# Twelve tiles of a feed-forward product in two blocks of seven products, added into DRAM by the output pairs

## The chip, the cores and the metric

The kernel runs on one core of one Trainium2 chip. The metric is the device time of one execution in microseconds (us); the median of three runs is compared. Engines are named as in the profile: PE is TensorE, PEld its weight loads, DVE is VectorE, ACT is ScalarE, POOL is GpSimd, SP is SyncE. SP and POOL both issue DMAs, each on a queue of its own (q1 for SP, q0 for POOL).

## The reference, cut to what matters

One layer of a diffusion backbone over 512 latent tokens of width 1024: a token mixer, a gated residual, then a SwiGLU feed-forward block (FFN) with a gated residual, and a last RMS norm. The change lies in the FFN alone:

```python
D_FF = -(-8 * D_MODEL // (3 * 256)) * 256        # 2816 = 22 tiles of 128

def _swiglu(h, w_in, w_out):
    g, u = jnp.split(h @ w_in, 2, axis=-1)
    return (jax.nn.silu(g) * u) @ w_out

x = x + g2 * _swiglu(_modulate(x, norm_ffn[l], sh2, sc2), w_ffn_in[l], w_ffn_out[l])
return _rmsnorm(x, norm_final)
```

The first product makes 22 tiles of g and 22 of u, the second sums the 22 tiles of silu(g) * u into 8 output tiles of 128 rows and 512 tokens.

## The kernel before, in words

Activations lie with channels on the 128 partitions and the 512 tokens along the free axis. To keep fp32 accuracy each operand is split into a high and a low fp32r half, and a product of two tiles is three matmuls: high by high, high by low, low by high (`mm3`, lines 191 to 193). `mm3_low_last` (L198 to L201) does the same sums with the low weights at the end.

**Block products.** A tile pair, g_j above u_j, by the 512 tokens in two halves of 256 is a 2 x 2 block product. It is done with seven block products instead of eight, in the manner of Strassen and Winograd, from sums of weight blocks (A11, S1, S2, A12, S3, S4, A22) and sums of the token halves (11, N1, N2, 21, T3, 22, T4). Class `Pair` issues them: `front` does A11, S1, S2, A12, and `back` does S3, S4, A22. With 8 tiles of input width each block product is 4 x 3 matmuls of 256 columns, 84 for a pair. Between A11 and S2 ScalarE copies one PSUM bank to another (L1091).

`prepare` makes a pair's weights ready: two loads by SP, into `ur` (two buffers, L1021) and `wr` (three buffers, L1022), then sums on DVE (L1054 to L1062), casts and splits on ACT and DVE (L1034, L1036, L1044, L1045). Blocks named in `sent` get their low half another way: ACT writes the negated high half (L1038) and an accumulating DMA on POOL's queue adds the weight from DRAM (`ol<-in_wffi`, L1039). `Even` and `Odd` are pairs whose results are not only split but also summed and split again, so that two tiles of silu(g) * u serve as the block operand of the second product; there are three buffers (`bo`) for three such double tiles. `Out` is a pair of output tiles: the seven block products of two of the eight output rows by six tiles, 7 x 3 x 3 = 63 matmuls of 256 columns. Its results are scaled by the gate and written to DRAM by POOL's queue (L1247, L1251).

`run` interleaves the items: while one item's front runs, the back of the item before is woven in, and the next item's weights are prepared. Where an Out follows an Odd (`joint`), the order is different, since the Out's operands are only just being made. Outside the parts with an order written by hand (`manual_schedule`), a planner orders each engine's instructions; `issue_after` holds one back until another has been issued.

**Stages of the FFN before.**

1. Tiles 0 to 2 as plain products, then pairs 3 to 7.
2. First part of the second product: each of 8 output tiles sums tiles 0 to 7, 24 matmuls of 512 columns, with weights of 1024 columns loaded, cast and split (`wchunk`, L161, L162). The result is added to the residual `x1` (L1432), and x1 goes to the DRAM tile `x1d` (L1455, L1470).
3. Even and Odd pairs for tiles 8 to 13, then four Outs. An Out writes into the DRAM tile `od`.
4. Plain pairs 14 to 21. Meanwhile `also` adds od to x1d, row by row, by accumulating DMAs from DRAM to DRAM on POOL's queue (L1487).
5. The tail: x1 is read back from x1d (L1524), each output tile sums tiles 14 to 21 in two token halves, 24 matmuls of 256 columns each, and squares are summed (L224 to L231) for the last norm, which multiplies (L1514) and stores.

The last pair's tile is put off in stage 2 and in the tail: output 0 (in the tail the first two) begins with the other tiles.

Of the kernel before, what the change touches and what calls it, by code (L numbers as in the profile page):

```python
# [10 lines left out]
F32 = mybir.dt.float32  # L11
F32R = mybir.dt.float32r
AF = mybir.ActivationFunctionType
ALU = mybir.AluOpType
# [3 lines left out]
P = 128  # L18
D = 1024
KT = D // P  # L20
T = 512
# [29 lines left out]
def layer_kernel(ctx: ExitStack, tc, xT, cT, w0, w1, wv0, wv, wada_a, wada_b, par, crow, bg, wpool,  # L51
                 wout, wffi, wffo, icnt, consts, out):
    nc = tc.nc
# [7 lines left out]
    def open_pool(name, tags, side="left"):  # L61
        st = ExitStack()
        p = st.enter_context(tc.tile_pool(name=name, bufs=1, side=side, reuse_waits="tile"))
        pools[name] = p
        for t in tags:
            homes[t] = p
        stacks[name] = st

    def close_pool(name):
        stacks.pop(name).close()  # L70

    def tl(tag, shape, dtype=F32, bufs=1, align=None):
        cnt[0] += 1
        return homes[tag].tile(shape, dtype, name=f"{tag}_{cnt[0]}", tag=tag, bufs=bufs, align_bytes=align)

    def S(tag, dtype=F32):
        return tl(tag, [P, T], dtype, bufs[tag], HALFLINE if tag in shifted else LINE)

    ps = ctx.enter_context(tc.tile_pool(name="ps", bufs=4, space=PSUM))
    dram = ctx.enter_context(tc.tile_pool(name="dram", bufs=1, space=DRAM))  # L80
# [127 lines left out]
    class SumSq:  # L208
# [4 lines left out]
        def __init__(self, urgent=()):  # L213

            self.urgent = urgent
            self.n = {}
            self.last = {}
# [58 lines left out]
    def mod_rows(k):  # L276

        raw = tl("ada", [P, KT, 256], F32, 3)
        nc.sync.dma_start(raw.rearrange("p k c -> p (k c)"), wada_a[k])
        acc = PS()  # L280
        for r in range(2):
            for g in range(4):
                nc.tensor.matmul(acc[32 * g:32 * g + 32, :256], sil[:, 4 * r + g, :], raw[:, 4 * r + g, :],
                                 start=r == 0, stop=r == 1, tile_position=(0, 32 * g))
        rows = S("tmp")
        nc.scalar.copy(rows[:, :256], acc[:, :256])
        return rows
# [83 lines left out]
    rows = mod_rows(0)  # L371
# [5 lines left out]
    rows = mod_rows(1)  # L377
# [5 lines left out]
    for k in range(KT):  # L383
        parts = ((0, 0), (0, 1), (1, 0))[0 if k else 1:]
        products(k, 0, nf // 2, parts)
        if k + 2 < KT:
            rows = mod_rows(k + 2)
# [598 lines left out]
    def norm_tiles(c, r, at, also=lambda k: None):  # L986
        t = norm_first(0, c, r)
        for k in range(KT):
            t = norm_rest(k, c, t, at(k), lambda: norm_first(k + 1, c, r) if k < KT - 1 else None)
            also(k)  # L990
# [80 lines left out]
    class Pair:  # L1071
# [5 lines left out]
        begun, f, behind = False, None, None  # L1077
# [53 lines left out]
        def second(self, y):  # L1131
            s = self.s[:, TC:]
            nc.scalar.activation(s, y, AF.Silu)
            V.scalar_tensor_tensor(s, self.q[:, TC:], -1.0, s, ALU.mult, ALU.mult)

        def fourth(self, x):
            s = self.s[:, :TC]
            V.scalar_tensor_tensor(s, x, -1.0, s, ALU.mult, ALU.mult)
            self.done()
# [73 lines left out]
    class Out(Pair):  # L1213
# [3 lines left out]

        def __init__(self, j, turn, evens, c0, c1):
            super().__init__(j, turn)
            self.evens, self.c, self.into = evens, slice(c0 * P, c1 * P), od[c0]  # L1220

        def prepare(self):
            w = [wffo[2 * self.j + e][:, self.c] for e in range(2)]
# [20 lines left out]

        def second(self, y):
            self.scaled(self.o[:, TC:], y, g2)
            nc.gpsimd.dma_start(self.into[2 * self.j], self.o)  # L1247

        def fourth(self, x):
            self.scaled(self.o1[:, :TC], x, ng2)  # L1250
            nc.gpsimd.dma_start(self.into[2 * self.j + 1], self.o1)  # L1251

    def made(it):
        for _ in it.prepare():
# [2 lines left out]
    def run(items, also=lambda it: None):  # L1257

        prev, casts[:] = None, []
        for it, after in zip(items, items[1:] + [None]):  # L1260
            f = it.f = it.f or it.front()
            if after:
                made(after)
            b = prev.back() if prev else iter(())
            joint = isinstance(it, Out) and not isinstance(prev, Out)
            if joint:
                next(b)
            if not it.begun:
                next(f)
                if joint:  # L1270
                    next(b)
                next(f)
            if casts:
                with tc.issue_after(it.copied.ins):
                    casts.pop().cast(0, 4)
            if joint:
                next(b)
                after.f = after.front()
                next(after.f)
                next(after.f)  # L1280
                after.begun = True
            next(b, None)
            next(f)
            next(b, None)
            next(f)
            next(b, None)
            also(it)
            prev = it
# [2 lines left out]
    ng2 = small([P, KT], "ng2")  # L1291
    V.tensor_scalar(ng2, g2, -1.0, None, ALU.mult)
    x1d = dram.tile([KT, P, T], F32, name="x1d")
    od = {c0: dram.tile([KT, P, T], F32, name=f"od{c0}") for c0 in (8,)}

    for j in range(NW, KT):
        proj_out(j, wo[j], HALF[0])
# [51 lines left out]
    with tc.manual_schedule(engines={mybir.EngineType.PE, mybir.EngineType.Activation, mybir.EngineType.DVE}):  # L1349
# [7 lines left out]
        f = Half(1, HALF[0])  # L1357
# [19 lines left out]
        f = Half(1, HALF[1])  # L1377
# [20 lines left out]
        f = Half(2, HALF[1])  # L1398
# [42 lines left out]

    starts = (8,)
    turn = itertools.count(NP + 1)
    plain = [third] + [Pair(j, next(turn)) for j in range(NP + 1, starts[0])]
    plain[1].behind = third.p["low"]
# [3 lines left out]
    c1 = starts[0]  # L1451
# [4 lines left out]
    items, ins = [], []  # L1456
    for c0 in starts:
        evens = []
# [6 lines left out]
    c0, c1 = starts[-1] + 6, FT  # L1465
    plain = [Pair(j, next(turn)) for j in range(c0, c1)]
# [4 lines left out]
    close_pool("late4")  # L1471
    close_pool("late0")
    open_pool("late0", ("bo", "nf", "ev"))
    rows = iter([(c, j) for c in starts for j in range(KT)])

    def also(it):
        if it is plain[0]:
            close_pool("late0")
            open_pool("late0", ("act", "before_act", "x1"))
            tl("before_act", [P, NEXT], F32, 1, LINE)  # L1480
            shifted.add("act")
            bufs["act"] = 2 * (c1 - c0)
            x1[:] = [S("x1") for _ in range(KT)]
        if it in plain[:-2]:
            with tc.issue_after(items[items.index(it) + 1].p["added"].ins):
                for c, j in itertools.islice(rows, 1 + (it in plain[1:3])):
                    nc.gpsimd.dma_start(x1d[j], od[c][j], accum_op=ALU.add, max_dma_last_dim=2048)  # L1487

    for _ in run(items, also=also).back():
        pass  # L1490
# [145 lines left out]
```

## Time and profile before

| what | value |
|---|---|
| median of 3 runs | 884.06 us (883.71 to 884.94) |
| the profiled execution's own time | 883.43 us |
| its span, first to last instruction | 881.6 us |
| PE busy | 870.8 us (99%) |
| DVE, ACT, POOL busy | 631.2, 454.2, 82.6 us |
| first part of the second product (tiles 0 to 7) | 616.9 to 660.4 us |
| Even and Odd pairs and Outs (tiles 8 to 13) | 660.4 to about 754 us |
| plain pairs 14 to 21, up to the tail | up to 826.5 us |
| tail, up to the last residual's product | 826.5 to 871.1 us |
| DMA: mean rate, and POOL's queue q0 | 147 GB/s; 8032 packets, 16.26 MB |

Times in the profile count from the first instruction. "L1091" is line 1091 of the kernel. In the view of windows a row gives a stretch, its length, the busy time and count of each engine in it, the granted clock, the mean busy share of the 16 DMA engines and the rate. In a timeline a row is start, duration, engine, line, operation, out<-in, and in brackets the idle time before and what ended it. The starts of two matmuls in a row tell their pace, as they overlap.

### The profile page before, as it was taken

The page shows a single profiled execution, that of the slowest core. Times are in us where ns is not written, and L with a number is a line of the kernel's source. Part 1 is how long each engine was busy: PE and PEld are TensorE (multiplying, and loading weights), DVE is VectorE, ACT ScalarE, POOL GpSimd, SP SyncE. Part 2 cuts the span into 40 slices and gives each one's busy share as a digit, 9 for nine tenths or more (in the row PEclk, how much of TensorE's full clock was granted, in tenths as well). Part 3 has the DMA queues.
Part 4 walks back from the last instruction along what each step waited for, and adds up shares of the span by engine and source line. Part 5 has one row for each costly group of instructions (what it writes and reads, how often), then busy time and mean ns, then how long its engine had stood idle before and what let it go on. Part 6 is the DMA issues. An engine that isn't in the chain of part 4 may idle for free.

```text
span 881.6 us, 15517 instructions
## 1 busy us (share of the span) xinstructions
PE 870.8 (99%) x6052; PEld 800.4 (91%) x6052; DVE 631.2 (72%) x1232; ACT 454.2 (52%) x867; POOL 82.6 (9%) x117
## 2 busy tenths in 40 slices
PE   9999999999999999999999999999999999999996
PEld 8689798899888998889988899999889999999996
DVE  5678677867876688767886667794376898786544
ACT  4464354455344453445454447674146768676431
POOL 0000010020000100000000000020011202322000
PEclk9999999999999999999999999999999999999999
DMA  9853021436252542434354740385476647998502
GB/s 352 326 194 112 25 72 60 169 106 181 72 185 91 152 158 83 148 112 140 127 162 130 266 141 1 89 211 133 131 207 171 150 108 213 219 227 204 168 1 96
DMA packets 45449, 129.83 MB, mean 147 GB/s; under 512 B 5024, under 2 KB 9408, under 8 KB 44352
## 3 DMA queue, kind: packets, MB, share of 16 engines
q1 hardware_dynamic: 37344, 112.59, 39.4%
q0 software_dynamic: 8032, 16.26, 9.5%
q8 instruction: 47, 0.77, 0.3%
q14 instruction: 26, 0.21, 0.1%
HBM read 120.94 MB, written 9.98 MB: 149 GB/s over the span
## 4 chain that ended last, share of the span: by engine, by line
PE 89%; DMA 3%; ACT 2%; DVE 2%; issue 2%; DVEq 0%; POOLq 0%; POOL 0%; SPq 0%; ACTq 0%
PE ps L191 12%; PE ps L192 12%; PE ps L193 12%; PE ps L201 8%; PE ps L199 8%; PE ps L198 8%; PE pat L351 3%; PE ps L582 3%; PE ps L583 3%; PE ps L584 3%; PE pat L192 2%; PE pat L193 2%; PE pat L191 2%; PE pat L796 2%; PE pat L797 2%
## 5 line engine op out<-in xcount | busy, mean ns | idle before, releaser
L161 ACT CAST wh<-wr 128x1024 fp32r<-128x1024 f32 (+2 forms) x70 | 71.8, 1025 | 83.0 <-PE ps L199 34.8
L162 DVE TENSOR_TENSOR wl<-wr,wh 128x1024 fp32r<-128x1024 f32 (+2 forms) x70 | 84.2, 1203 | 34.6 <-ACT wh L161 22.6
L198 PE MATMUL ps<-a,wh 128*128 128x512 f32 x272 | 106.6, 392 | 0.0
L199 PE MATMUL ps<-a,wh 128*128 128x512 f32 x272 | 106.3, 391 | 0.0
L201 PE MATMUL ps<-a,wl 128*128 128x512 f32 x272 | 68.0, 391 | 0.0
L199 PEld LDWEIGHTS ps<-a,wh 128*128 128x128 f32 x272 | 51.1, 188 | 10.2
L201 PEld LDWEIGHTS ps<-a,wl 128*128 128x128 f32 x272 | 50.9, 188 | 10.5
L198 PEld LDWEIGHTS ps<-a,wh 128*128 128x128 f32 x272 | 51.1, 188 | 10.1
L191 PE MATMUL ps<-act,wh 128*128 128x256 f32 (+1 forms) x155 | 51.5, 332 | 0.0
L193 PE MATMUL ps<-act,wl 128*128 128x256 f32 (+1 forms) x155 | 51.3, 331 | 0.0
L192 PE MATMUL ps<-act,wh 128*128 128x256 f32 (+1 forms) x155 | 51.3, 331 | 0.0
L191 PE MATMUL ps<-hp,gh 128*128 128x256 f32 x176 | 49.6, 282 | 0.8 <-ACT pat L1091 0.5
L193 PE MATMUL ps<-hp,ol 128*128 128x256 f32 x176 | 48.9, 278 | 0.7 <-DVE ol L1036 0.7
L1039 POOL DMA_DIRECT2D ol<-in_wffi x40 | 35.5, 897 | 145.9 <-ACT tmp L1126 62.9
L191 PE MATMUL ps<-hp,oh 128*128 128x256 f32 x176 | 49.0, 278 | 0.1
L192 PE MATMUL ps<-hp,gh 128*128 128x256 f32 x176 | 49.0, 278 | 0.0
L193 PE MATMUL ps<-hp,gl 128*128 128x256 f32 x176 | 48.9, 278 | 0.0
L192 PE MATMUL ps<-hp,oh 128*128 128x256 f32 x176 | 48.8, 277 | 0.0
L541 DVE SCALAR_TENSOR_TENSOR pb<-pb,crow_s 128x1024 f32<-128x1024 f32 x32 | 38.9, 1234 | 10.9 <-DMA pb<-in_wada_b 10.8
L796 PE MATMUL pat<-vh,Sp 128*128 128x258 f32 x144 | 41.1, 286 | 0.0
L797 PE MATMUL pat<-vl,Sp 128*128 128x258 f32 x144 | 40.7, 283 | 0.0
L798 PE MATMUL pat<-vh,Sp 128*128 128x258 f32 x144 | 40.7, 282 | 0.0
(421 smaller groups left out, 2870.3 us busy)
## 6 DMA issues: line engine op xcount, KB each, us to landing
wr<-in_w SPq DMA_DIRECT2D x42, 512.0 KB, 3.6
pb<-in_wada_b SPq DMA_DIRECT2D x32, 512.0 KB, 4.2
wr<-in_wffi SPq DMA_DIRECT2D x25, 512.0 KB, 4.2
ol<-in_wffi POOLq DMA_DIRECT2D x40, 256.0 KB, 6.0
ur<-in_wffi SPq DMA_DIRECT2D x19, 512.0 KB, 4.0
ada<-in_wada_a SPq DMA_DIRECT2D x8, 1024.0 KB, 10.4
wr<-in_wffo SPq DMA_DIRECT2D x16, 512.0 KB, 4.0
wr<-in_wout SPq DMA_DIRECT2D x8, 512.0 KB, 3.5
```

What stands on the lines that cost most here:

```text
L161: nc.scalar.copy(wh, raw[:, :n])
L162: V.tensor_sub(wl, raw[:, :n], wh.bitcast(F32))
L191: nc.tensor.matmul(dst, wh, ah, start=first and i == 0, stop=False, skip_group_check=on)
L192: nc.tensor.matmul(dst, wh, al, start=False, stop=False, skip_group_check=on)
L193: nc.tensor.matmul(dst, wl, ah, start=False, stop=last and i == n - 1, skip_group_check=on)
L198: nc.tensor.matmul(dst, wh, ah, start=first and i == 0, stop=False)
L199: nc.tensor.matmul(dst, wh, al, start=False, stop=False)
L201: nc.tensor.matmul(dst, wl, ah, start=False, stop=last and i == len(wparts) - 1)
L541: V.scalar_tensor_tensor(wa[:, :D], wa[:, :D], 0.5, crow_s, ALU.mult, ALU.mult, accum_out=mods[:, i:i + 1])
L796: nc.tensor.matmul(o, sh_, vh[:, s, :], start=n == 0, stop=False)
L797: nc.tensor.matmul(o, sh_, vl[:, s, :], start=False, stop=False)
L798: nc.tensor.matmul(o, sl_, vh[:, s, :], start=False, stop=n == len(srcs) - 1)
```

## The change

Tiles 0 to 4 stay plain in front and 17 to 21 behind. Tiles 5 to 16 form two blocks of six, 5 to 10 and 11 to 16, each with its three Even and Odd pairs and its four Outs. The Outs of both blocks add their results straight into x1d by an accumulating DMA from SBUF; the DRAM tile od and the later additions of od into x1d are gone. The weights of stage 2 and of the tail are then 640 columns wide per output tile instead of 1024.

```diff
@@ class Out @@
-            self.evens, self.c, self.into = evens, slice(c0 * P, c1 * P), od[c0]
+            self.evens, self.c = evens, slice(c0 * P, c1 * P)
@@ def second @@
-            nc.gpsimd.dma_start(self.into[2 * self.j], self.o)
+            nc.gpsimd.dma_start(x1d[2 * self.j], self.o, accum_op=ALU.add)
@@ def fourth @@
-            nc.gpsimd.dma_start(self.into[2 * self.j + 1], self.o1)
+            nc.gpsimd.dma_start(x1d[2 * self.j + 1], self.o1, accum_op=ALU.add)
...
-    od = {c0: dram.tile([KT, P, T], F32, name=f"od{c0}") for c0 in (8,)}
...
-    starts = (8,)
+    starts = (5, 11)
...
-    rows = iter([(c, j) for c in starts for j in range(KT)])
@@ def also @@
-        if it in plain[:-2]:
-            with tc.issue_after(items[items.index(it) + 1].p["added"].ins):
-                for c, j in itertools.islice(rows, 1 + (it in plain[1:3])):
-                    nc.gpsimd.dma_start(x1d[j], od[c][j], accum_op=ALU.add, max_dma_last_dim=2048)
```

## The prediction, made before the change was run

> **What bounds the kernel now.** I read the page first: its busy shares, its queue rows and the chain that ended last.
>
> ```profile
> PE 870.8 (99%) x6052; PEld 800.4 (91%) x6052; DVE 631.2 (72%) x1232; ACT 454.2 (52%) x867; POOL 82.6 (9%) x117
> PE 89%; DMA 3%; ACT 2%; DVE 2%; issue 2%; DVEq 0%; POOLq 0%; POOL 0%; SPq 0%; ACTq 0%
> ```
>
> TensorE is busy for 870.8 of 881.6 us and carries 89% of the chain, so fewer matmuls shorten the kernel unless a wait takes their place. A share over the whole span can't tell where such a wait would come. I therefore cut the feed-forward part into its stages with the view of windows (first column the stretch, then its length, then busy time and count of PE, PEld, DVE, ACT, POOL, then clock, DMA share and GB/s).
>
> ```profile
> 616.92:660.40 43.48, 43.48 (x194) 36.05 (x193) 24.82 (x31) 14.37 (x19) 6.00 (x9) 1.00 0.55 168
> 661.00:715.93 54.93, 54.93 (x477) 54.74 (x477) 44.11 (x76) 37.77 (x70) 9.56 (x11) 1.00 0.65 150
> 715.93:726.54 10.61, 10.55 (x90) 10.35 (x88) 10.02 (x24) 7.86 (x18) 0.00 (x0) 1.00 0.38 119
> 729.60:743.88 14.28, 14.28 (x129) 14.28 (x127) 12.55 (x21) 10.98 (x23) 3.12 (x5) 1.00 0.70 225
> 744.90:768.47 23.57, 23.10 (x197) 22.69 (x196) 17.30 (x26) 17.36 (x34) 9.37 (x13) 1.00 0.89 226
> 768.47:806.91 38.44, 38.44 (x339) 38.44 (x337) 30.26 (x48) 26.17 (x48) 11.89 (x14) 1.00 0.92 198
> 826.53:871.06 44.53, 44.53 (x394) 44.53 (x393) 21.76 (x41) 16.82 (x37) 0.71 (x1) 1.00 0.16 53
> ```
>
> In order these are: tiles 0 to 7 of the second product; the Even and Odd pairs 8 to 13; the joint, where the first Out follows the last Odd; two full Out periods; the passage from the last Out to the plain pairs; four plain pairs; the tail with tiles 14 to 21. PE fills all of them but two: the joint and the passage. There is no slack to win elsewhere, and what the change duplicates is exactly those two.
>
> The pace of a 256-column matmul is read from two rows of the timeline, 17 matmuls apart; the 512-column pace is the first window over its 192 matmuls, 0.2265 us.
>
> ```profile
> 599.75 0.28 PE L191 MATMUL pat<-hp,wh 128*128 128x256 f32 x1
> ...
> 601.68 0.28 PE L193 MATMUL pat<-hp,ol 128*128 128x256 f32 x1
> ```
>
> (601.68 - 599.75) / 17 = 0.1135; two Out periods of 63 give 14.28 / 126 = 0.1133, which I use.
>
> **The change part by part.**
>
> *Products.* The first part loses tiles 5, 6, 7: 8 outputs x 3 tiles x 3 terms = 72 matmuls of 512 columns, 72 x 0.2265 = -16.31 us. The tail loses tiles 14, 15, 16: 8 x 2 halves x 3 x 3 = 144 of 256 columns, 144 x 0.1133 = -16.32. Four more Outs of 63 add 252 x 0.1133 = +28.55. Sum -4.08 us, the whole gain: seven block products for eight.
>
> *Six plain pairs (5, 6, 7, 14, 15, 16) become Even or Odd.* They have the same 84 matmuls, but VectorE and ScalarE also form and split four sums. That work hides under PE: in 661.00:715.93 DVE was busy 44.11 of 54.93 and PE never stopped. I cost it at 0. If the cover goes (the second block starts with less work prepared ahead), up to +1.0: a tenth of a 9.6 us pair (38.44 / 4) each time DVE is late.
>
> *A second joint.* 715.93:726.54 holds 87 matmuls, 87 x 0.1133 = 9.86 us of 10.61: +0.75 for another one.
>
> *A second passage out of Outs*, now from Out 3 of the first block into an Even. 744.90:768.47 holds 195 matmuls: 168 of pairs at 38.44 / 336 = 0.1144 and 27 of Outs at 0.1133, together 22.28 of 23.57, so 1.29 us are lost. Out periods last 7.14 us and the next pair's preparation wants a pair's 9.6. An Even's loads, casts and sent accumulations before its products are a Pair's: +1.3. Ends: 0.5 if the planner places the copies better, 1.6 if also the pace suffers.
>
> *Output pairs add into x1d at once.* Per Out two plain writes into od become two accumulating DMAs, 16 in all, and the eight od to x1d transfers under the plain pairs go. POOL's issues cost little (9% busy). An accumulation of the second block into a row must come after that of the first block into it, some 86 us earlier (six pairs and four Outs): no wait. On the queue, POOL's pairs of issues keep their places, and behind them stand the accumulations into ol that PE needs a period or more later. What changes is the DMA engines' work in the passage. Its place is found by following the second stall there:
>
> ```profile
> 744.66 0.56 POOL L1247 DMA_DIRECT2D od<-tmp  x1 [2.49 <-ACT tmp L1234]
> 745.71 0.88 POOL L1039 DMA_DIRECT2D ol<-in_wffi  x1 [0.49 <-ACT ol L1038]
> 746.43 0.71 POOL L1251 DMA_DIRECT2D od<-tmp  x1
> ```
>
> ```profile
> 745.43 5.28 DMA ur<-in_wffi
> ```
>
> ```profile
> 750.81 0.69 DVE L1054 TENSOR_TENSOR sg<-ur 128x512 f32<-128x512 f32 x1 [1.96 <-DMA ur<-in_wffi]
> 758.02 0.39 ACT L1091 COPY pat<-ps 128x256 f32<-128x256 f32 x1
> 758.46 0.39 PE L191 MATMUL ps<-hp,gh 128*128 128x256 f32 x1 [0.30 <-ACT pat L1091]
> ```
>
> The first fence is POOL's timeline, the second the chain of waits, the third DVE, ACT and PE from their timelines. The ur load of the pair after next starts when its buffer comes free at 745.43, takes 5.28 us among POOL's transfers, DVE waits for it, ScalarE's queue behind it is late, and L1091, which must empty the bank before product S2, ends 758.41: PE stops. Whatever makes that load later, PE pays. No row shows an accumulation from SBUF into DRAM. Nearest rows, by what the 16 engines moved while busy (windows with a plain od write alone, an ol accumulation alone, and od to x1d mixed with ol):
>
> ```profile
> 756.00:756.90 0.90, 0.90 (x10) 0.90 (x9) 0.89 (x2) 0.90 (x3) 0.66 (x2) 1.00 0.67 269
> 672.65:674.10 1.45, 1.45 (x15) 1.45 (x14) 0.94 (x2) 1.13 (x2) 0.00 (x0) 1.00 0.76 136
> 769.00:771.00 2.00, 2.00 (x20) 2.00 (x19) 1.83 (x4) 0.72 (x1) 0.01 (x1) 1.00 1.03 136
> ```
>
> 262 KB at 269 / 0.67 = 401 GB/s is 0.65 us; at 136 / 0.76 = 179 it is 1.46; at 136 / 1.03 = 132 it is 1.99. The new transfer reads SBUF and DRAM and writes DRAM; I take 1.46, the row with one side in each memory, so +0.8 per transfer, ends 0 and +1.35. One of them (744.66) goes in front of the load on the chain: +0.8 per passage, two passages, +1.6. Ends: 0 where the load slips past, 2 x 1.35 = 2.7 per passage where both writes of the Out stand before it, +5.4.
>
> The Trainium skill, Collectives: The Full Stack, section The bandwidth ceiling: the fold count and why AG ≠ RS ≠ AR, says that an added-in transfer costs not by its add but because it reads two sources for one write, twice a copy. By that, twice 0.65 is 1.3 us (an estimate), +0.65 per transfer, and the sum below would be 0.3 us lower. This trace's ol row is 2.2 times a plain write, so I keep the row.
>
> *The end of the last pair.* Before, od to x1d transfers run until x1 is read back, and DVE was late for it:
>
> ```profile
> DVE gl L181 <- DMA x<-x1d: 2.3, 1, 2.3
> ```
>
> ```profile
> 824.67 0.28 PE L193 MATMUL pat<-hp,wl 128*128 128x256 f32 x1
> 825.05 0.39 PE L191 MATMUL ps<-hp,oh 128*128 128x256 f32 x1
> ```
>
> The first fence is a row of the waits, the second PE's timeline: two matmuls start 0.38 apart, 0.27 too much. After, x1d is complete some 47 us earlier (five pairs) and the weight loads are 320 KB instead of 512: -0.3, ends -0.4 and 0.
>
> *Less cover in the two shortened parts.* The first part runs 4 tiles of output 0 before it needs the last pair's tile, 12 x 0.2265 = 2.72 us in place of 4.76. ScalarE's and DVE's timelines give when that tile is made:
>
> ```profile
> 618.71 0.62 ACT L1142 CAST act<-tmp 128x512 fp32r<-128x512 f32 x1 [1.68 <-DVE tmp L1138]
> ```
>
> ```profile
> 616.78 1.23 DVE L162 TENSOR_TENSOR wl<-wr,wh 128x1024 fp32r<-128x1024 f32 x1 [1.69 <-ACT wh L161]
> ...
> 619.36 0.69 DVE L1143 TENSOR_TENSOR act<-tmp,act 128x512 fp32r<-128x512 f32 x1 [0.69 <-ACT act L1142]
> ```
>
> From the part's start at 616.92 the high half is there after 2.41 us, in time, and the low half after 3.13, wanted at 2.72 + 0.23 = 2.95. The weight split of 1.23 us ahead on DVE shrinks to five eighths of its columns, some 0.4 us. Cost 0, end +0.3. In the tail a slot of 24 matmuls (2.72 us) becomes 15 (1.70). The last slots are where it shows:
>
> ```profile
> 865.81 1.22 DVE L1514 TENSOR_TENSOR ur<-ur,pat 128x1024 f32<-128x1024 f32 x1
> 866.95 0.42 DVE L231 TENSOR_TENSOR tmp<-tmp,tmp 128x256 f32<-128x256 f32 x1
> 867.28 1.22 DVE L1514 TENSOR_TENSOR ur<-ur,pat 128x1024 f32<-128x1024 f32 x1
> 868.54 0.48 DVE L1432 SCALAR_TENSOR_TENSOR x<-ps,lb,x 128x256 f32<-128x256 f32 x1
> ```
>
> These 3.2 us of DVE fitted beside two slots of 5.4 and now stand beside 3.4, so the last sums start late: +0.25, ends 0 and +0.5.
>
> **Sum.** -4.08 + 0 + 0.75 + 1.3 + 1.6 - 0.3 + 0 + 0.25 = -0.5 us. The profiled execution took 883.43 us (span 881.6); the median of the runs is 884.06, 0.63 above it. On the profiled time the sum gives 882.9, on the median 883.5, my prediction. A difference under 0.2% (1.8 us) can't be told from no change here.
>
> **The rivals.**
>
> *Loads slip past the accumulations (faster).* Then the +1.6 goes, and with the better end of the passage (0.5) the sum is -4.08 + 0.75 + 0.5 - 0.3 + 0.25 = -2.9: 881.2 us. For it: under the plain pairs the DMA share was 0.92, yet PE did not stop between 768.47 and 806.91. Against it: the 5.28 us above, with only plain writes and one accumulation around it. The Trainium skill, DMA: Bandwidth & Descriptors, section Queues, rings and completion order, has each DMA engine take turns between rings, a packet at a time, by which a load of SP's ring waits for one packet of POOL's and not for all of them. That speaks for this rival; the 5.28 us agree with it only in part.
>
> *Accumulations hold up the loads (slower).* Both writes of an Out stand before the ur load, each 1.35 longer: 2.7 per passage. Without the accumulations' term the sum is -2.1; with 5.4 it is +3.3: 887.4 us. It decides from (1.8 + 2.1) / 2 = 1.95 us per passage. For it: DMA share 0.89 in the passage already, with 0.7 in the Outs; against it: one pair later the copy L1091 was done 0.37 us before PE wanted it.
>
> ```profile
> 767.73 0.37 ACT L1091 COPY pat<-ps 128x256 f32<-128x256 f32 x1
> 768.47 0.28 PE L191 MATMUL ps<-hp,gh 128*128 128x256 f32 x1
> ```
>
> *DVE falls behind in the second block.* Even and Odd after Outs rather than after the light first part, +1.0: 884.5, still within the bound.
>
> **How the numbers follow.** No measurable change 0.42 (the sum, or the sum with the DVE rival), faster 0.31 (loads slip past), slower 0.27 (loads held up). The likeliest's own range is 882.3 to 885.8. The range 881.0 to 887.4 takes in most of the faster case and the slower one's price, leaving one in ten on either side.
>
> **What would show it.** Right: 36 matmuls of 256 columns less in sum, the first part near 27.2 us, the tail near 28; twice a joint of some 0.7 us; in both passages ur loads of 5.5 to 7 us and L1091 as what PE waits for, 2 us each; no wait at the last pair's end. Wrong: passages that lose 1.3 or less (loads slip past) or over 3 (held up), PE waiting among the second block's Evens and Odds, or POOL waiting for a landing before it issues an accumulation into x1d.

## The result, and the profile after

The changed kernel takes 891.06 us (median of 4 runs, 890.62 to 891.61), the kernel before 883.88 (883.35 to 884.94): ratio 1.0083, 95% interval 1.0069 to 1.0096. It is slower by 7.2 us (0.8%), where 883.5 was predicted, no change that can be told. The profiled execution took 891.32 us with a span of 889.5, 7.9 above the span before.

First the page of the changed kernel: the busy shares, the span's chain by engine, and the row of DMA issues for the pairs' second weight load (count, KB each, median us from issue to landing); under them the same DMA row of the kernel before.

```profile
PE 872.7 (98%) x6088; PEld 801.9 (90%) x6088; DVE 652.4 (73%) x1292; ACT 472.4 (53%) x919; POOL 87.4 (10%) x119
PE 82%; DMA 5%; DVE 5%; ACT 4%; issue 2%; DVEq 0%; ACTq 0%; SPq 0%
ur<-in_wffi SPq DMA_DIRECT2D x19, 512.0 KB, 5.5
```

```profile
ur<-in_wffi SPq DMA_DIRECT2D x19, 512.0 KB, 4.0
```

There are 36 matmuls more by count, since 512-column matmuls became 256-column ones (72 fewer of the first, 108 more of the second). A 512-column matmul lasts as long as two, and counted so they are 36 of 256 columns fewer, as predicted. TensorE's share of the chain fell from 89% to 82%, and DMA, VectorE and ScalarE took it. The ur load's median grew by 1.5 us. The stages, in the view of windows of the changed kernel: first part; the entry (the first Even and Odd pairs); two Out periods; the passage out of the first block; the passage out of the second; the tail.

```profile
587.53:614.74 27.21, 27.21 (x122) 22.53 (x121) 17.17 (x25) 11.08 (x17) 6.03 (x9) 1.00 0.56 173
614.74:644.03 29.29, 28.23 (x239) 27.61 (x238) 23.05 (x38) 18.50 (x34) 5.22 (x6) 1.00 0.84 212
678.09:692.37 14.28, 14.28 (x126) 14.10 (x125) 12.13 (x25) 10.15 (x22) 1.75 (x2) 1.00 0.56 141
699.84:737.00 37.16, 34.92 (x293) 33.75 (x292) 27.76 (x45) 25.47 (x51) 11.02 (x13) 1.00 0.89 204
791.05:836.00 44.95, 42.39 (x354) 41.32 (x353) 29.06 (x45) 28.21 (x56) 11.46 (x13) 1.00 0.81 186
848.10:878.25 30.15, 29.68 (x251) 29.16 (x249) 19.08 (x38) 14.59 (x36) 0.97 (x1) 1.00 0.11 34
```

The first part and the Out periods have the predicted lengths (27.2 and 7.14 us) with PE busy throughout. Time is lost at the entry, in both passages and in the tail. What PE waited for, from 600 us on (total, times, longest), before and then after:

```profile
PE ps L191 <- ACT pat L1091: 0.5, 2, 0.3
```

```profile
PE ps L191 <- ACT pat L1091: 5.3, 9, 1.1
PE ps L191 <- DVE tmp L1129: 0.4, 1, 0.4
PE ps L192 <- DVE act L1143: 0.3, 1, 0.3
```

A fuller measure is the excess of the starts of two matmuls over their pace (0.1133 us at 256 columns, 0.2266 at 512), where it is above 0.05. I call it a stall; all stalls after 540 us come to 5.2 us before and 14.9 after, each in the one execution that was profiled.

| place | before | after | added | predicted to add |
|---|---|---|---|---|
| products | | | -4.1 | -4.08 |
| entry | 0.26 | 1.9 | +1.6 | 0 |
| joints | 0.34 | 0.66 + 0.34 | +0.7 | +0.75 |
| passages | 1.02 | 3.85 + 4.05 | +6.9 | +1.3 + 1.6 |
| end of the last pair | 0.38 | none | -0.4 | -0.3 |
| tail, its one long stall | none | 1.02 | +1.0 | +0.25 |
| pace (excess up to 0.05 each) | 3.3 | 5.25 | +2.0 | not counted |

The first row is worked out, the others are measured. The sum is +7.7 us of the 7.9. The pace is partly the tail again: 848.10 to 878.25 is 30.15 us where the prediction's terms give 44.53 - 16.32 + 0.25 = 28.46, 1.7 more, of which the long stall is 1.0.

### The profile page after: what moved, and what is told of

Same layout as the page of the kernel before. It is cut to its first block, busy times and chain, and to the rows that moved or that the text cites. A ratio compares the mean times of both kernels' runs of the same rounds, so it can differ in the third digit from the quotient of the medians.

```text
span 889.5 us, 15766 instructions
## 1 busy us (share of the span) xinstructions
PE 872.7 (98%) x6088; PEld 801.9 (90%) x6088; DVE 652.4 (73%) x1292; ACT 472.4 (53%) x919; POOL 87.4 (10%) x119
## 4 chain that ended last, share of the span: by engine, by line
PE 82%; DMA 5%; DVE 5%; ACT 4%; issue 2%; DVEq 0%; ACTq 0%; SPq 0%
PE ps L191 10%; PE ps L192 9%; PE ps L193 9%; PE ps L201 8%; PE ps L199 8%; PE ps L198 8%; DMA ur<-in_wffi 4%; PE pat L351 3%; PE ps L582 3%; PE ps L583 3%; PE ps L584 3%; PE pat L192 2%; PE pat L191 2%; PE pat L193 2%; PE pat L796 2%
## 5 line engine op out<-in xcount | busy, mean ns | idle before, releaser
L161 ACT CAST wh<-wr 128x1024 fp32r<-128x1024 f32 (+3 forms) x70 | 67.9, 969 | 70.8 <-PE ps L199 34.8
L162 DVE TENSOR_TENSOR wl<-wr,wh 128x1024 fp32r<-128x1024 f32 (+3 forms) x70 | 79.7, 1139 | 31.7 <-ACT wh L161 20.6
L201 PEld LDWEIGHTS ps<-a,wl 128*128 128x128 f32 x272 | 50.8, 188 | 10.5
L1044 ACT CAST gh<-sg 128x1024 fp32r<-128x1024 f32 (+1 forms) x27 | 26.7, 988 | 35.9 <-DVE sg L1055 21.8
L191 PEld LDWEIGHTS ps<-hp,gh 128*128 128x128 f32 x176 | 33.2, 188 | 7.9 <-ACT pat L1091 7.3
L192 PE MATMUL ps<-act,wh 128*128 128x256 f32 (+1 forms) x116 | 38.3, 331 | 0.3 <-DVE act L1143 0.3
```

Of the source, the lines that this page charges most:

```text
L161: nc.scalar.copy(wh, raw[:, :n])
L162: V.tensor_sub(wl, raw[:, :n], wh.bitcast(F32))
L191: nc.tensor.matmul(dst, wh, ah, start=first and i == 0, stop=False, skip_group_check=on)
L192: nc.tensor.matmul(dst, wh, al, start=False, stop=False, skip_group_check=on)
L201: nc.tensor.matmul(dst, wl, ah, start=False, stop=last and i == len(wparts) - 1)
```

## How one late load becomes a row of stalls

The chain of waits of the changed kernel behind the second block (start, length, what):

```profile
814.25 5.86 DMA ur<-in_wffi
820.20 0.70 DVE sg L1054
820.93 0.70 DVE sg L1055
821.71 1.06 ACT gh L1044
...
823.93 1.22 DVE wl L1045
...
825.41 0.68 DVE sg L1061
826.09 0.35 DVE tmp L1138
...
826.99 0.62 ACT oh L1034
...
828.04 0.37 ACT pat L1091
```

The weights land, VectorE sums S1 and S2, ScalarE casts, VectorE splits and sums again. L1091, the short copy that empties PE's bank, stands in ScalarE's queue behind these casts, and PE starts 0.66 us late:

```profile
828.45 0.39 PE L191 MATMUL ps<-hp,gh 128*128 128x256 f32 x1 [0.66 <-ACT pat L1091]
```

This chain is closed into a loop: the next load may start only when the casts from `ur` are done. The turn ahead of it, from the timelines of SP, VectorE, ScalarE and SP again:

```profile
803.84 0.33 SPq L1021 DMA_DIRECT2D ur<-in_wffi  x1
```

```profile
810.11 0.69 DVE L1055 TENSOR_TENSOR sg<-sg,wr 128x512 f32<-128x512 f32 x1
```

```profile
810.91 1.05 ACT L1044 CAST gh<-sg 128x1024 fp32r<-128x1024 f32 x1 [4.33 <-PE pat L193]
811.86 1.05 ACT L1044 CAST wh<-sg 128x1024 fp32r<-128x1024 f32 x1
813.09 0.61 ACT L1034 CAST oh<-ur 128x512 fp32r<-128x512 f32 x1
813.60 0.63 ACT L1038 ACTIVATE ol<-ur 128x512 fp32r<-128x512 f32 x1
```

```profile
814.25 0.33 SPq L1021 DMA_DIRECT2D ur<-in_wffi  x1
```

`ur` has two buffers, and the casts that end at 814.23 free the one of the load before, issued at 792.61. They are in the loop all the same, since they stand in ScalarE's queue behind `gh`, which is cast from the sums of the load of 803.84. These sums end at 810.80; the row of `gh` names PE, which was done with the old `gh` at about the same time.

From issue to issue are 10.41 us, 0.8 more than the 9.6 of a pair. The load of 803.84 landed at 809.29, after 5.45 us; sums and casts took the other 4.96. So a load over some 4.6 us (9.6 - 4.96, an estimate from this turn) makes the turn longer than a pair, and the next turn starts late as well. In the first passage of the changed kernel successive loads took 4.7, 6.3, 7.0 and 5.0 us, before 3.6, 5.3, 3.8 and 3.9: one load above the limit then, several now.

What lengthens them stands in the DMA view of the passages: q0 is POOL's queue, its last figure the share of 16 engines' time; then issues, count, KB and median us to landing. The changed kernel (694 to 730 us), then the two-block kernel without any accumulation into x1d (695 to 731 us, the first experiment):

```profile
q0 software_dynamic: 1852, 3.38, 58.1%
ur<-in_wffi SPq DMA_DIRECT2D x4, 512.0 KB, 5.7
x1d<-tmp POOLq DMA_DIRECT2D x6, 256.0 KB, 6.7
```

```profile
q0 software_dynamic: 1537, 3.51, 42.1%
ur<-in_wffi SPq DMA_DIRECT2D x4, 512.0 KB, 4.2
od<-tmp POOLq DMA_DIRECT2D x6, 256.0 KB, 2.9
```

POOL's queue moves slightly less and holds the engines for 16% of 36 us, 5.8 us, longer: about 1 us for each of six transfers. What one accumulating write takes is read from the DMA view of 786 to 788 us of the changed kernel. POOL's queue has nothing but such writes in flight there, and a load begins on SP's queue, q1 (packets, MB, share):

```profile
q0 software_dynamic: 131, 0.24, 88.3%
q1 hardware_dynamic: 19, 0.08, 10.4%
```

0.24 MB in 0.883 x 2 us is 136 GB/s, and 262 KB at that rate are 1.9 us; 1.46 was predicted, 0.65 is the plain write. By the Trainium skill, DMA: Bandwidth & Descriptors, section Queues, rings and completion order, each engine takes turns between queues by the packet. A load then waits once at each of its packets and not once in all. The rows above make SP's packets 4 KB and POOL's 0.22 us long (0.883 x 2 x 16 / 131); a load of 512 KB is 128 such packets, 8 for each engine if they are spread evenly, and 8 x 0.22 adds 1.7 us (an estimate). The shortest loads in these passages took 3.6 us, so taking turns alone would make them some 5.3: most of the way to the median of 5.7, and not to the 7.0. That longest load, of 701.39, also stood behind SP's own `wr` load of 697.75, which landed at 704.52. No view shows the engine of a packet, so the turns themselves are not shown.

## The experiments

Each kernel is compared with runs of the kernel before on the same chip. Differences of medians are in us; stalls are of the profiled execution. Runs of the two-block kernels scatter over 1 to 6 us, and a profile shows one of them, which may lie far from the median. So a difference of 1 or 2 us between two profiles is no proof by itself.

**Two blocks, nothing added.** In the changed kernel the Outs write plainly into one od tile per block and od is added nowhere, so the output leaves out the second product of tiles 5 to 16.

```diff
-            nc.gpsimd.dma_start(x1d[2 * self.j], self.o, accum_op=ALU.add)
+            nc.gpsimd.dma_start(self.into[2 * self.j], self.o)
```

> The changed kernel with its Outs writing plainly into a DRAM tile per block, as before; nothing adds those tiles to x1d, so the second product of tiles 5 to 16 is left out of the output. Theory A (accumulating writes slow the ur loads): both passages out of Outs lose about 1.3 us each as in the kernel before, the waits of PE for L1091 fall from 5.3 to about 1.5 us, time near 885. Rival B (the two-block order itself leaves preparation no lead, whatever an Out writes): the waits stay and the time stays at 889 to 891.

885.53 us against 883.54, ratio 1.0025 (1.0014 to 1.0036). Of the 7.2 us some 5 come with the accumulations; 2.0 stay without them. That agrees with the theory that accumulating writes slow the loads, and not with its rival. PE's waits for L1091 fell from 5.3 to 3.0 us, not to 1.5, and the passages stall 1.85 and 1.94 us, more than the 1.3 expected; the entry (2.0) and the tail (0.82) are as in the changed kernel.

**One block, Outs accumulate.** The kernel before with this one edit of Out, and od and its additions gone.

> The kernel before with one edit: its four Outs add straight into x1d, no od and no later additions. Theory A: its one passage loses 3 to 4 us more and the last pair's wait goes, 886.5 to 888. Rival B: same as before within 1 us, 883 to 885.

885.73 us against 883.54, ratio 1.0028 (1.0018 to 1.0037). This lies between the ranges of the theory and of the rival. The single passage grows from 1.02 to 3.5 us of stalls in a profile that took 888.46 us, the slowest of ten runs, so 3.5 is likely high; the 0.38 at the last pair's end goes. On the medians the accumulations cost 2.2 + 0.4 = 2.6 us in this passage, and 7.2 - 2.0 = 5.2 in the two of the changed kernel: as much here as in each of the two blocks. In the chain between 740 and 790 us of the kernel before, and between 745 and 795 of this one, the ur load's share more than doubles:

```profile
by line: PE ps L191 16.7%; PE ps L193 16.2%; PE ps L192 16.2%; DMA ur<-in_wffi 10.6%; PE pat L191 6.9%; PE pat L192 6.7%; PE pat L193 6.4%; ACT wh L1044 4.2%; issue 4.1%; ACT oh L1034 4.1%; ACT ol L1038 2.4%; ACT tmp L1234 1.7%; DVE sg L105
```

```profile
by line: DMA ur<-in_wffi 24.7%; PE ps L191 11.4%; PE ps L193 10.3%; PE ps L192 10.3%; issue 7.8%; PE pat L192 4.3%; PE pat L191 4.3%; ACT wh L1044 4.2%; PE pat L193 3.9%; ACT oh L1034 3.7%; ACT ol L1038 3.2%; DVE wl L1045 2.4%; ACT gh L1044
```

**Which of the accumulations.** Two kernels divide them: in the first only the last Out of each block accumulates, in the second only the first three; the others write plainly and are not added in, so their rows leave out the second product of tiles 5 to 16.

```diff
+            if self.j == 3:        # the other kernel: self.j < 3
                 nc.gpsimd.dma_start(x1d[2 * self.j], self.o, accum_op=ALU.add)
+            else:
+                nc.gpsimd.dma_start(od[self.c.start // P][2 * self.j], self.o)
```

> The changed kernel with the accumulation kept for the last Out of each block alone (output rows 6 and 7); the first three Outs write plainly into od, and nothing adds od in, so six output rows leave out the second product of tiles 5 to 16. With no accumulation at all it took 885.5 us, with all sixteen 891.1, so the place of 5.5 us is sought. If one load on the chain pays for the one transfer ahead of it, as the prediction has it, the last Out's writes carry nearly all: passages as in the changed kernel (3.9 us each) and 890 to 891 us. If every turn of the loop load, sums, casts, next load pays for the accumulations beside it, only the turns behind the last Out are longer: passages of 2.7 to 3 us each, 887.5 to 888.5 us.

> The counterpart: Outs 0 to 2 of each block accumulate into x1d, the last Out writes plainly into od and is not added in (rows 6 and 7 leave out the second product of tiles 5 to 16). One load on the chain: the passages are as without any accumulation (1.9 us each), 885.5 to 886.3 us. Every turn pays: passages near 3 us, 887.5 to 888.5 us, the rest of the 5.5 us that the kernel with the last Out alone does not show.

887.80 and 887.98 us against 882.67: ratios 1.0059 (1.0040 to 1.0078) and 1.0059 (1.0038 to 1.0080). Both lie between the 1.0083 of all accumulations and the 1.0025 of none. The load that the prediction followed, 745.43 in the kernel before, stands beside the writes of the third Out (744.66 and 746.43); the last Out writes at 755.19 and 756.87. So the first expectation has it the wrong way round: if that one load paid for all, the last Out alone would cost nothing and the first three alone everything. On the medians the last Out alone costs as much as the first three, and its interval lies above that of the kernel without accumulations. So the cost belongs to more than one load. The chain of the changed kernel's first passage has three of them, and PE's late starts:

```profile
686.96 4.73 DMA ur<-in_wffi
...
694.77 6.33 DMA ur<-in_wffi
...
705.28 0.39 PE ps L191
...
713.60 5.01 DMA ur<-in_wffi
...
726.77 0.39 PE ps L191
```

Between them, at 716.09, PE waits for L1091 behind the load of 701.39, the one that stands where the prediction's stood.

How the cost divides between the Outs is not shown. The stalls of the passages depend on the execution, as the profiles of seven two-block kernels tell; the last three are described further down. In us: the difference of the medians to the kernel before, that of the profiled run to its own median, the stalls of both passages, and the median of the four ur loads issued from 694 to 727.

| kernel | Outs that accumulate | median to before | profiled run to median | stalls | ur loads |
|---|---|---|---|---|---|
| nothing added | none | +2.0 | +0.9 | 1.9 + 1.9 | 4.2 |
| last Out | one of four | +5.1 | -0.6 | 1.9 + 2.5 | 4.5 |
| first three Outs | three of four | +5.3 | +0.9 | 3.0 + 2.8 | 4.4 |
| the changed kernel | all | +7.2 | +0.3 | 3.9 + 4.1 | 5.7 |
| three outputs begun in the tail | all | +7.2 | -3.0 | 2.0 + 4.4 | 5.3 |
| Even early, behind 1, 3, 4, 5 | all | +9.1 | -4.3 | 1.6 + 1.9 | 4.5 |
| Even early, behind 3, 4, 5, 6 | all | +6.6 | -2.6 | 2.7 + 2.5 | 5.0 |

With all Outs accumulating both passages together stalled between 3.5 and 7.9 us, less in runs that were fast for their kernel. So much of the scatter seems to lie there, and the 4.4 and 5.8 us of the two parts don't rank them. On the medians they add 3.1 and 3.3 us to the kernel without accumulations, all together add 5.2. A turn that is late already should pay for every further delay, and one that is in time absorb it; that is argued from the loop, and these runs don't show it.

**Plain writes, three times over.** The kernel before, with each Out write made three times: into od and into two spare tiles that nothing reads.

```diff
-            nc.gpsimd.dma_start(self.into[2 * self.j], self.o)
+            for d in (self.into, *spare):
+                nc.gpsimd.dma_start(d[2 * self.j], self.o)
```

> The kernel before (one block) with each of an Out's two plain writes made three times, to od and to two spare DRAM tiles: 3 x 0.65 = 1.95 us of DMA time, as much as one accumulating write takes, with no accumulation. Theory: only the DMA engines' time counts, so the passage loses what e2's did, 885 to 886. Rival: the accumulation's own order or packets count, plain writes slip between the loads, 883.5 to 884.3.

889.77 us against 883.45, ratio 1.0076 (1.0058 to 1.0093). The same 291 matmuls of the passage, from the first product of the plain pairs on, took 34.57 us in the kernel before (744.90 to 779.47), and so long where the one block's Outs accumulate and where they write plainly three times:

```profile
747.61:785.09 37.48, 35.11 (x293) 34.27 (x292) 27.45 (x42) 23.70 (x46) 10.25 (x12) 1.00 0.87 194
```

```profile
745.76:783.45 37.69, 35.15 (x293) 34.19 (x292) 25.07 (x38) 23.62 (x46) 17.66 (x25) 1.00 0.98 269
```

That is 2.9 and 3.1 us more. Plain traffic does as much harm, so nothing peculiar to an accumulation is needed for it, and time on the shared engines fits as the cause. It isn't a clean equivalent: here the writes also held their `tmp` buffers (15.5% of this passage's chain is `DMA od<-tmp`), and the last pair's end stalls 1.94 us behind tail weights, which is part of why the median lies above the 885 to 886 that were expected. In the changed kernel's chain from 690 to 740 us no DMA but the ur load stands, so the hold on `tmp` is not what delays it there.

**The rival: VectorE short.** The changed kernel with the low half of A22 made by VectorE, not by ScalarE and an accumulating load: one accumulation per pair less on the queue, 0.69 us of VectorE more.

```diff
-        sent = ("A12", "A22")
+        sent = ("A12",)
-                self.sent = ("A11", "A12", "A22")
+                self.sent = ("A11", "A12")
```

> The changed kernel with the low half of block A22 subtracted on VectorE as A11's is, not sent through an accumulating DMA: one accumulation of about 1.5 us of DMA time less per pair, one DVE instruction of 0.69 us more and one ACT instruction of 0.63 us less. Theory A (accumulating DMAs delay the ur loads, and these close the loop ur load, sums, casts, ur free): ur loads in the passages land in 4 to 5 us instead of 5 to 7, 2 to 4 us less: 887 to 889. Rival (VectorE is what is short in a passage): slower than the changed kernel, 892 or more.

900.45 us against 883.45, ratio 1.0192 (1.0174 to 1.0210). The waits of PE from 600 us on:

```profile
PE ps L191 <- ACT pat L1091: 4.2, 4, 1.6
PE ps L191 <- DVE tmp L1242: 3.6, 2, 2.5
PE ps L191 <- DVE tmp L1129: 1.6, 1, 1.6
```

The ur loads of the first passage hardly became shorter (4.72, 5.53, 7.05 and 4.81 us). VectorE is part of the loop, and the added time shows in good part as waits for it. Relieving the queue at VectorE's cost is a bad bargain: 9.8 us more than the changed kernel on these medians. In the changed kernel itself PE does not wait between 737 and 763 us, among the second block's Evens and Odds, so that rival did not come by itself.

**The entry.** One kernel keeps the first part long (blocks at 8 and 14, eight tiles in front, two behind). Two others keep blocks 5 and 11 and prepare the first Even within the first part, step by step behind outputs 1, 3, 4, 5 or behind 3, 4, 5, 6.

```diff
-    starts = (5, 11)
+    starts = (8, 14)
```

> The changed kernel with blocks at tiles 8 to 13 and 14 to 19, so that the first part keeps its 8 tiles and the tail has 2. The same products. If the first Evens wait because the first part is short (2.2 us lost there), that loss falls to about 0.4 us; the tail's slots of 6 matmuls (0.7 us) are shorter than VectorE's and ScalarE's work for a slot (0.9 us), so the tail loses 4 us or more: 891 to 894. If the short first part isn't the reason, the loss at the first Evens stays at 2 us.

895.91 us against 883.54, ratio 1.0142 (1.0123 to 1.0161). The entry's stalls are 0.26 us as before the change, so the shortened first part makes that stall. But with two tiles behind, the last pair's end and the tail starve, by more than was expected:

```profile
PE ps L191 <- DVE tmp L1129: 4.6, 1, 4.6
PE pat L241 <- DVE tmp L231: 2.7, 1, 2.7
```

```diff
+        if j in (1, 3, 4, 5):      # the other kernel: (3, 4, 5, 6)
+            next(early)            # one step of items[0].prepare()
```

> The changed kernel with the first Even's preparation written into the first part (loads after output 1, A11 with S1 and S2 after output 3, A12 after 4, the sums after 5) instead of behind it. If the first Evens wait for a late preparation, 1 to 2 us of the 2.2 lost there come back, 889 to 890. If the DMA engines are what is late there, nothing changes.

> As e4_early_even, with the first Even's preparation written two outputs later (loads after output 3, then after 4, 5 and 6). In e4 the loss at the first Evens fell to 0.3 us but the first part lost 3.1 us at its start, because the Even's loads took the place of its own. Theory: later loads keep both, the first part loses under 1 us and the first Evens under 1 us, 889 to 890 beside 891 for the changed kernel. Rival: three buffers and one queue serve both, so what one gains the other loses, 891.

892.65 us against 883.54 and 890.06 against 883.45: ratios 1.0096 (1.0065 to 1.0127) and 1.0075 (1.0048 to 1.0102). Neither is told apart from the changed kernel. In both the entry's 1.9 us fall to 0.26, and other stalls take their place: 2.5 us just ahead of the first part in the first kernel (PE waits for VectorE's L1129, behind a pair's weight load of 7.9 us), 1.9 us near the first part's end in the second (PE waits for that part's own weights). The work is moved, not hidden: 27 us of first part cover less preparation than 43 did.

**The tail.** The changed kernel with three outputs begun without the last tile instead of two.

```diff
-    first = [ffn_bank()[:, :T] for _ in range(2)]
+    first = [ffn_bank()[:, :T] for _ in range(3)]
```

> The changed kernel with three outputs instead of two begun in the tail before the last pair's tile is wanted: 36 matmuls of cover (4.1 us) for 24 (2.7 us). Theory: the 1.0 us stall at the tail's first slot is the last tile being late behind weight casts, so it goes: 0.5 to 1.0 us less than the changed kernel, 890.1 to 890.6. Rival: the tail's loss is the weight loads themselves, then the wait only moves to the fourth output and the time stays.

890.60 us against 883.45, ratio 1.0085 (1.0068 to 1.0102). In the profile the tail's 1.02 us stall is gone and PE is busy 28.00 of 28.00 us from 848 to 876; the median is 7.2 us above the kernel before as without the edit, and these runs lie between 887.6 and 892.2. The cause of the stall is shown, the gain isn't.

**Where else to add.** Two attempts at a better version. One has two blocks, plain writes, and 16 additions from od into x1's tiles in SBUF in the tail, with three outputs begun. The other is the kernel before with its eight additions moved there. In essence (the first kernel goes through both blocks' od):

```diff
                     nc.sync.dma_start(x1[i], x1d[i])
+                for i in range(KT):
+                    nc.gpsimd.dma_start(x1[i], od[c][i], accum_op=ALU.add)
```

> The changed kernel with plain writes of all Outs into one od per block, and both blocks' rows added in the tail, by 16 accumulating DMAs from DRAM into x1's tiles in SBUF behind the read back of x1; and three outputs begun in the tail instead of two. Same output as the reference. Without any adding in, the two blocks took 885.5 us; the tail's share of DMA was 0.16, 16 accumulations at 1.46 us are 23.4 us of 28. If they fit beside the tail's products, and the third begun output takes most of the tail's 1.0 us stall, 884.7 us. If rows come late, PE waits in the tail by a few us: 888 to 890.

> The kernel before with its eight rows of od added not into x1d under the plain pairs but into x1's tiles in SBUF in the tail. Under the loop theory the first pairs behind the Outs have lighter company (two to three fewer transfers of 2 us beside their loads): the passage's 1.0 us falls to 0.8 or less, and the 0.38 us at the last pair's end goes: 883.0 us. If the plain pairs' loads were hidden anyway and the tail's rows come late: 884 to 885.

893.49 and 889.43 us against 882.67: ratios 1.0115 (1.0089 to 1.0141) and 1.0078 (1.0058 to 1.0098), both slower than any case that was expected. The additions weren't spread over the tail; they went out as soon as x1 landed, in the second kernel between 810 and 819 us with the tail's first product at 830, beside the tail's weight loads. DMA issues between 812 and 832 us there:

```profile
wr<-in_wffo SPq DMA_DIRECT2D x4, 512.0 KB, 6.0
x<-od POOLq DMA_DIRECT2D x7, 256.0 KB, 11.1
```

In the kernel before such a weight load takes 3.7 us. It is the same fault as in the passages, at another place: PE waits 3.1 us at the last pair's end. No kernel of these beat the one before. Additions held back until the tail's weights have landed, casts of A22 ahead of `gh` in ScalarE's queue, and a third `ur` buffer were not tried.

## Why the prediction was wrong

- *Products, -4.08.* Right: first part 27.2 us, Out period 7.14, pairs at their pace where nothing waits.
- *Second joint, +0.75.* Right: the 87 matmuls of the two joints take 10.56 and 10.62 us, 0.7 and 0.76 over their pace.
- *End of the last pair, -0.3.* Right: the 0.38 us stall is gone.
- *Accumulations, +0.8 per passage.* This step failed: "One of them (744.66) goes in front of the load on the chain: +0.8 per passage". The path, a late ur load that makes ScalarE's L1091 late, was the right one, and the transfer was only somewhat undersized (1.9 us for 1.46, so 1.0 to 1.3 more than a plain write and not 0.8). But the count of one transfer ahead of one load was wrong. Six accumulating writes stand in a passage, several loads in a row are held up, and each makes PE late: +2.6 us per passage on the medians. Behind the load that was followed the stall grew from 0.6 us to 1.4 in the first passage, the forecast 0.8, and to 1.0 in the second; the load after it, which cost nothing before, added 0.7 and 0.9, and in the second passage the next one 0.9 more. That 0.8 came out once is luck: without any accumulation the stall was 1.0 in the first experiment. The rival with both writes in front (+2.7 per passage) came nearer, by number if not by mechanism: the passages' stalls grew by 2.0 and 2.1 us over the same kernel without accumulations.
- *Second passage without accumulations, +1.3.* Undersized: 1.85 and 1.94 us in the first experiment, +2.8 for both over the one of 1.02; why it is more was not isolated. The stall of a passage varies by itself: the kernel before with its additions moved to the tail had 0.2 us there, and its transfers up to that point were the same.
- *Six pairs become Even or Odd, 0, and the first part's cover, 0.* The entry added 1.6 us, above both ends (+1.0 and +0.3). The prediction looked at the act tile and the first weight split, and not at the next pairs' loads: the ur load of the block's third pair started 10.5 us ahead of the entry before (649.87) and 3.7 us ahead after (611.01); that of the fourth came 2.7 us behind it and took 3.8 us before (663.14), and came 4.4 us behind and took 8.7 us after (619.15).
- *Tail, +0.25.* Undersized: 30.15 us are 1.9 over 44.53 - 16.32. That the last act tile is there nearly in time was worked out for output 0 of the first part alone; in the tail its low half ended at 851.8, behind weight splits on VectorE, and the two begun outputs of 12 matmuls lasted only until 850.8.
- *What was said to show it.* Passages that lose "over 3 (held up)" were named as a sign of being wrong, and they came (3.9 and 4.1 us of stalls); so did ur loads of 5.5 to 7 us and waits for L1091. POOL never waited for a landing, as predicted.

Left open: the 2.0 us of pace. In parts of this execution matmuls start 4% further apart with a granted clock of 1.00 (861.37 to 871.97: six products of 15 in 10.60 us, 0.1178 each, against 0.1133 in the tail before). Some of it may be short waits below the bound of 0.05; no run isolates it.

## What to carry to other kernels

A buffer that is refilled by a load, used, and freed for the next load is a loop, and its turn has to be compared with the period of the work that it feeds: here 5.0 us of sums and casts plus the load, against 9.6 us. A second buffer doesn't open the loop where an engine's queue puts the work that frees it behind work that waits for the newest load. Once the turn is longer than the period, a delay is handed on, so price the whole stretch's DMA time and not the one transfer beside one load. And a part that is shortened loses the cover that it gave to the preparation behind it: count all the loads that used to start in it.

## What the runs showed of the hardware

An accumulating write of 262 KB from SBUF into DRAM took 1.9 us of the 16 engines, at 136 GB/s, while a load took a tenth of their time; that is 2.9 times a plain write's 0.65. By the Trainium skill, Collectives: The Full Stack, section The bandwidth ceiling: the fold count and why AG ≠ RS ≠ AR, two reads for one write would make it twice (an estimate, 1.3 us); the measured ratio is higher.

PE's granted clock can halve after a pause. In the kernel before with its additions in the tail, PE stood from 824.1 to 827.2 us, and then had (first row; the second is from blocks 8 and 14, after a pause of 4.6 us):

```profile
827.20:831.00 3.80, 3.77 (x19) 3.78 (x20) 2.67 (x5) 3.14 (x6) 0.00 (x0) 0.55 0.93 243
```

```profile
862.40:866.00 3.60, 3.60 (x17) 3.60 (x18) 1.52 (x4) 1.16 (x4) 0.00 (x0) 0.50 0.20 59
```

Matmuls of 256 columns then started 0.21 us apart for 3.6 us, which adds some 1.7 us to the 3.1 us of the pause. After a pause of 3.29 us in the two blocks with additions in the tail the clock stayed at 1.00, while one of 3.13 us had halved it, so the length of the pause alone doesn't decide.

The Trainium skill, TensorE: Matmul & The Clock Gate, Part 1, has the clock halved after an idle window of about 3.4 us, in windows that run freely and not from the pause's start. That the longer of two pauses did nothing agrees with free-running windows; the 3.13 us that were enough are a little below the page's figure, and the starts of the two matmuls around them, 823.82 and 827.23, lie 3.41 apart.
